# Two transformer layers in one launch: more output products by pairs with seven block products, q and k by tokens, transposes later

## The chip, the cores and the metric

The program runs on one core of a Trainium2 chip. The metric is the device time of one launch in microseconds (us). Inputs and the result are f32 in HBM; every weight is read once.

## The reference, cut to what matters

A hybrid layer and then a second layer, for 256 tokens of width 2048:

```
proj = rms_norm(x, g_mix) @ w_in            # qa, ka, va, qr, kr, vr, gr, gate_a, gate_r
oa   = attention(rms_norm(heads(qa), q_gain), rms_norm(heads(ka), k_gain), heads(va))   # 8 heads of 128
orr  = head_group_norm(retention(qr, kr, vr)) * silu(gr)                                # 4 heads
merged = sigmoid(gate_a) * (oa @ w_o_attn) + sigmoid(gate_r) * (orr @ w_o_ret)
x = x + merged @ w_out
g, u = split(rms_norm(x, g_ffn) @ w_ffn_in)           # 2 x 5632
x = x + (silu(g) * u) @ w_ffn_out
# second layer
x = x + rms_norm(token_mixer(rms_norm(x)), attn_post_norm)
a, b = split(rms_norm(x) @ w_ffn_in_2)                # 2 x 5632
x = x + rms_norm((gelu(conv3(a)) * b) @ w_ffn_out_2, ffn_post_norm)
```

## The kernel before, in words

Every large product is made in three parts: an f32 operand is split into a high part (a rounded copy, type f32r) and a low part (the rest), and high x high, high x low and low x high are added in PSUM. Activations are kept split and transposed (`hx1`, `orr`, `mg`, `hx2`, `act`, `hx3`, `hx4`). Weights come from HBM by SyncE in blocks of 128 x 1024 (512 KB) through four buffers (`wraw`), and each block is split on its way: ScalarE copies the high part (L113), VectorE subtracts it for the low part (L115). `Sched` does this in the order of the tasks: each task calls `take()` once a block, which loads six blocks and splits four blocks ahead of TensorE. After each block comes `tick()`: it runs what `later(n, ...)` has put n steps ahead, and one step of each of two lists of generators (attention, retention and the like). So the whole order of the work on every engine is written out at build time, and each engine keeps that order.

Kinds of tasks: **V** takes a block of 256 rows of weights x 512 columns with the activations as stationary operand and makes two token tiles of 512 columns, 12 products of 512 columns a block (L1261 to L1263). **T** takes the weights as stationary operand and makes 128 features of all tokens, so a product of 512 columns (high and low of the activations side by side) and one of 256 for each 128 rows (L1388, L1390). **B** and **W** keep the blocks' parts and do one token tile after the other, with other work hung between the blocks ("hooks"); W has 256 columns a product. **S** (`pair_products`) takes two groups of 512 columns, left and right, at a time: four accumulators `c11` to `c22`. A block in the order with mark `True` uses a scheme with 7 products of 128-row blocks in place of 8: `p1`, `p5`, `p6`, `p7` are four more accumulators in the other four PSUM banks, sums of activations (`comb`) meet sums of weights, which VectorE makes from the two raw blocks in `sums()` (four operations of 512 columns, L145 to L149) and which are split like a block. Only the first FFN's input product (`w_f1`, 11 pairs with 3 such blocks each, order `ORDER`) is of this kind.

PSUM has eight banks, four under the tag `acc` and four under `m`. A pair's accumulators come from one tag and the four `p` from the other, by turns.

Around the change: `qk_evac` takes q's and k's features, makes their squares, and a step later `stats()` sums them with products of one column (L535); `attention()` makes the factors from it, spreads k's over 128 partitions with two transposes a head (`bcast`, L426) and scales k. `turned()` transposes row tiles `wait` steps after it is called (2 if nothing is said), four 128 x 128 transposes (L465) a half. `x4_row`, `x4_turn`, `x4_low` are the hooks that add the second mixer's result to x (VectorE), transpose it (TensorE, then four high parts on ScalarE) and make the low parts (VectorE). The FFNs' 44 row tiles go in two parts, `PARTS` = groups 0 to 5 and 6 to 10: input product, then output product of those groups, added into `x1` (`row_add`) or `ff` (`f_out`). The last output group of the second FFN is made as W over the second part (20 rows of weights of 128), so that the first token tile's result can be finished under the second one's products (`out_row`).

Large activations live in 15 slots of 8 KB a partition; `t512` has six buffers of 512 columns.

Of the kernel before, what the change touches and what calls it, by code (L numbers as in the profile page):

```python
# [11 lines left out]
F32 = mybir.dt.float32  # L12
# [14 lines left out]
PARTS = ((0, 6), (6, NG))  # L27
# [201 lines left out]
def body(ctx, tc, A, out):  # L229
# [141 lines left out]
    def pair_blocks(arr, a, b, order):  # L371

        blks = []
        for c, seven in order:
            left, right = [arr[g, c].rearrange("p a b -> p (a b)") for g in (a, b)]
# [3 lines left out]
    def pairs_of_groups(arr, of, order, lhs, comb, gate, done, first):  # L379

        blks = [b for x, y in of for b in pair_blocks(arr, x, y, order)]
        tasks.append(("S", blks, (len(of), order, lhs, comb, gate, done, first)))
# [84 lines left out]
    def turned(key, f0, srcs, use=None, then=None, gain=None, wait=2, comb=()):  # L467

        def part(j):
            def fn():  # L470
                m = mtile()
# [22 lines left out]
    def combine(key, i, m, gain):  # L494

        y, s = t512("y"), t512("s4")
        for n in range(2):
            copy(y[:, cols(n, S)], m[:, cols(n, S)], gain[n])
        a11, a21, a12, a22 = [y[:, cols(n, P)] for n in range(4)]
# [8 lines left out]

    def comb_of(key):
        return lambda i, n: st[("comb", key)][i // 2][:, i % 2, :, cols(n, P)]  # L510


    hx1 = rhs_of("hx1")

# [5 lines left out]
    st["qks"] = None  # L520

    def qk_evac(key, f, base):
        def evac(acc):
            y = st[key][:, f]
            total(y, acc)
            yield "post"
            sq = tmp.tile([P, S], F32, name="sq", tag="sq", bufs=2)
            nc.scalar.activation(sq, y, AF.Square)

            def stats():  # L530
                if st["qks"] is None:
                    st["qks"] = mtile()
                for k in range(2):
                    c = base + 2 * f + k
                    nc.tensor.matmul(st["qks"][:, c:c + 1], sq[:, k * P:(k + 1) * P], ones[:, 0:1],  # L535
                                     start=True, stop=True)
            q.later(1, stats)
        return evac
# [18 lines left out]
    for f in range(8):  # L557
        T(A["w_qa"], f, hx1, qk_evac("qa", f, 0))
    for f in range(8):
        T(A["w_ka"], f, hx1, qk_evac("ka", f, 16))  # L560

    def attention():
        yield
        yield
        r = nx.r
        r2 = small(2, "r2")
        tt(r2, r, r, ALU.mult)
        f32t = small(32, "qkf", 1)
        ms = small(32, "qkm", 1)
        tt(pairs(ms, 16), pairs(st["qks"][:, :32], 16), r2[:, None, :].to_broadcast([P, 16, 2]), ALU.mult)  # L570
        root(f32t, ms, 128)
        gqk = small(1, "gqk", 1)
        stt(gqk, gains["qk_norm"][:, 0:1], SC128, gains["qk_norm"][:, 1:2], ALU.mult, ALU.mult)
        yield
        yield
        tt(pairs(f32t, 16), pairs(f32t, 16), r[:, None, :].to_broadcast([P, 16, 2]), ALU.mult)
        yield
        st["oa"] = [slot([P, 4, 2, S], F32R, name="oa") for _ in range(2)]
        for h in range(A_HEADS):
            m = bcast(f32t[:, 16 + 2 * h:18 + 2 * h])  # L580
            kh = t256("kh")
            stt(kh, st["ka"][:, h], gqk, m[:, :S], ALU.mult, ALU.mult)
            yield
            p, rs = yield from softmax_rows(st["qa"][:, h], kh, f32t[:, 2 * h:2 * h + 2], -(2.0 ** -(h + 1)))
# [115 lines left out]
    def gr_evac(g):  # L700
        def evac(accs):
# [7 lines left out]
            turned("orr", 4 * g, sg, wait=1)  # L709
        return evac  # L710

    C(lambda: new_h("orr"))
# [14 lines left out]
    def ret_out(g):  # L727
        def evac(accs):
# [4 lines left out]
            turned("mg", 4 * g, sr)  # L733
        return evac

    C(lambda: new_h("mg"))
    for g in range(4):
        V(A["w_ga"], g, hx1, gate_evac("sa", AF.Sigmoid, nx))
        V(A["w_gret"], g, hx1, gate_evac("sr", AF.Sigmoid, nx))
# [25 lines left out]
    SEVEN = (0, 1, 2)  # L765
# [6 lines left out]

    for a, b in PARTS:
        C(lambda n=b - a: new_h("act", n))
        pairs_of_groups(A["w_f1"], [(j, NG + j) for j in range(a, b)], ORDER, rhs_of("hx2"), comb_of("hx2"), n1, "act",
                        (b - a) % 2)
# [298 lines left out]
    def x4_low(k, g):  # L1075
# [4 lines left out]
        (1, 0): [more], (1, 1): [(x4_row, 0, 0)], (1, 2): [(x4_turn, 0, 0), more], (1, 3): [(x4_row, 0, 1), (x4_low, 0, 0)],  # L1080
        (1, 4): [(x4_turn, 0, 1), more], (1, 5): [(x4_row, 0, 2), (x4_low, 0, 1)], (1, 6): [(x4_turn, 0, 2), more],
        (1, 7): [(x4_row, 0, 3), (x4_low, 0, 2)]}, cs=MIX)
    x4_hooks = {
        (0, 0): [(x4_turn, 0, 3)], (0, 1): [(x4_low, 0, 3)], (0, 2): [(x4_row, 1, 0)],
        (0, 3): [(x4_turn, 1, 0), (x4_row, 1, 1)], (0, 4): [(x4_low, 1, 0), (x4_turn, 1, 1)],
        (0, 5): [(x4_row, 1, 2), (x4_low, 1, 1)], (0, 6): [(x4_turn, 1, 2), (x4_row, 1, 3)],
# [42 lines left out]
    def f2_evac(key, j, use, then):  # L1129
# [63 lines left out]
    for a, b in PARTS:  # L1193
# [7 lines left out]
        if a == 0:  # L1201
            C(start_ff)
# [329 lines left out]
```

## Time and profile before

| | us |
|---|---|
| three runs | 2743.81, 2744.10, 2744.53 (median 2744.1) |
| profiled execution | 2742.58, of which the span 2740.8 |
| TensorE busy | 2708.5 (99%), 12777 matmuls |
| VectorE busy | 1689.7 (62%) |
| ScalarE busy | 1355.4 (49%) |
| DMA | mean 187 GB/s |

Busy time of TensorE is made of matmuls that overlap, their ends are modelled. Start-to-start times on its timeline tell what one costs. "Idle before" and "waits" count only time in which the engine had nothing running.

### The profile page before, as it was taken

What the parts mean: (1) busy time and instruction counts of PE and PEld (TensorE: products, weight loads), DVE (VectorE), ACT (ScalarE), POOL (GpSimd) and SP (SyncE); (2) the same over time, 40 slices, a digit from 0 to 9 for tenths busy, and PEclk for the clock granted to TensorE, in tenths of its full rate; (3) what the DMA queues carried; (4) which work ended last, traced back from release to release, by engine and by line L of the source; (5) the groups of instructions that cost most, each with busy time, mean ns of one, the idle gap of its engine ahead of it and who ended that gap; (6) DMA issues with size and microseconds to landing.
All of it is one profiled execution on the core that took longest, in us unless ns stands there. A gap on an engine that the chain in (4) does not pass through costs nothing.

```text
span 2740.8 us, 33567 instructions
## 1 busy us (share of the span) xinstructions
PE 2708.5 (99%) x12777; PEld 2253.2 (82%) x12777; DVE 1689.7 (62%) x2033; ACT 1355.4 (49%) x1759; POOL 59.5 (2%) x61
## 2 busy tenths in 40 slices
PE   8999999999999999999999999999999999999998
PEld 7888788888888887888888888888778888888887
DVE  5456555554467898648886557775555554455555
ACT  5445444444455555435555455554455554455543
POOL 0000000000000000000000001110000000000000
PEclk9999999999999999999999999999999999999999
DMA  8554456555555555655656565445555555555554
GB/s 276 175 181 163 160 171 215 194 189 196 191 177 195 179 200 191 209 194 182 207 184 204 183 210 168 145 152 191 177 177 184 185 185 191 192 191 185 185 189 142
DMA packets 142227, 511.42 MB, mean 187 GB/s; under 512 B 16945, under 2 KB 17329, under 8 KB 141553
## 3 DMA queue, kind: packets, MB, share of 16 engines
q1 hardware_dynamic: 140832, 502.71, 55.6%
q0 software_dynamic: 1088, 6.55, 0.6%
q8 instruction: 100, 1.64, 0.2%
q14 instruction: 63, 0.51, 0.1%
q10 hardware_dynamic: 144, 0.01, 0.0%
HBM read 507.11 MB, written 2.10 MB: 186 GB/s over the span
## 4 chain that ended last, share of the span: by engine, by line
PE 82%; DVE 8%; DMA 4%; issue 3%; ACT 2%; POOL 0%; DVEq 0%; ACTq 0%; POOLq 0%
PE acc L1263 21%; PE acc L1261 21%; PE acc L1262 21%; PE acc L1388 8%; DVE wlo L115 4%; PE acc L1390 4%; DMA wraw<-in_w_f 3%; PE m L465 1%; ACT whi L113 1%; DVE u L277 1%; PE acc L1286 1%; PE acc L1287 1%; PE acc L1288 1%; DVE sums L145 1%; DVE sums L146 1%
## 5 line engine op out<-in xcount | busy, mean ns | idle before, releaser
L115 DVE TENSOR_TENSOR wlo<-wraw,whi 128x1024 fp32r<-128x1024 f32 (+1 forms) x934 | 1119.3, 1206 | 802.6 <-ACT whi L113 798.7
L113 ACT ACTIVATE whi<-wraw 128x1024 fp32r<-128x1024 f32 (+1 forms) x934 | 966.6, 1041 | 788.3 <-PE acc L1263 675.0
L1261 PE MATMUL acc<-whi,hx 128*128 128x512 f32 x1456 | 581.7, 400 | 7.1 <-ACT hx L274 5.3
L1262 PE MATMUL acc<-wlo,hx 128*128 128x512 f32 x1456 | 568.4, 390 | 1.2 <-DVE wlo L115 1.2
L1263 PE MATMUL acc<-whi,hx 128*128 128x512 f32 x1456 | 569.3, 391 | 0.0
L1388 PE MATMUL acc<-hx,whi 128*128 128x512 f32 x912 | 330.6, 404 | 0.0
L1261 PEld LDWEIGHTS acc<-whi,hx 128*128 128x128 f32 x1456 | 274.0, 188 | 64.3 <-ACT hx L274 5.3
L1262 PEld LDWEIGHTS acc<-wlo,hx 128*128 128x128 f32 x1456 | 274.2, 188 | 58.8 <-DVE wlo L115 2.4
L1263 PEld LDWEIGHTS acc<-whi,hx 128*128 128x128 f32 x1456 | 273.8, 188 | 58.5
L1261 PE MATMUL acc<-whi,act 128*128 128x512 f32 (+1 forms) x704 | 271.1, 385 | 0.0
L1263 PE MATMUL acc<-whi,act 128*128 128x512 f32 (+1 forms) x704 | 269.8, 383 | 0.0
L1262 PE MATMUL acc<-wlo,act 128*128 128x512 f32 (+1 forms) x704 | 269.8, 383 | 0.0
L1390 PE MATMUL acc<-hx,wlo 128*128 128x256 f32 x912 | 255.7, 280 | 0.0
L1388 PEld LDWEIGHTS acc<-hx,whi 128*128 128x128 f32 x912 | 171.3, 188 | 38.9 <-issue 0.5
L1390 PEld LDWEIGHTS acc<-hx,wlo 128*128 128x128 f32 x912 | 172.4, 189 | 1.0 <-issue 0.5
L1263 PEld LDWEIGHTS acc<-whi,act 128*128 128x128 f32 x704 | 132.3, 188 | 26.1
L1261 PEld LDWEIGHTS acc<-whi,act 128*128 128x128 f32 x704 | 132.3, 188 | 25.7
L1262 PEld LDWEIGHTS acc<-wlo,act 128*128 128x128 f32 x704 | 132.4, 188 | 25.4
L113 ACT ACTIVATE whi<-sums 128x1024 fp32r<-128x1024 f32 x66 | 68.9, 1057 | 112.6 <-DVE sums L146 72.9
L1286 PE MATMUL m<-whi,hx 128*128 128x512 f32 x291 | 113.8, 391 | 0.0
L1288 PE MATMUL m<-whi,hx 128*128 128x512 f32 x291 | 113.3, 389 | 0.0
L1287 PE MATMUL m<-wlo,hx 128*128 128x512 f32 x291 | 113.3, 389 | 0.0
(332 smaller groups left out, 3047.9 us busy)
## 6 DMA issues: line engine op xcount, KB each, us to landing
wraw<-in_w_f SPq DMA_DIRECT2D x352, 512.0 KB, 3.4
wraw<-in_w_f1o SPq DMA_DIRECT2D x88, 512.0 KB, 4.2
wraw<-in_w_f2o SPq DMA_DIRECT2D x78, 512.0 KB, 3.3
wraw<-in_w_ga SPq DMA_DIRECT2D x34, 512.0 KB, 3.3
wraw<-in_w_vr SPq DMA_DIRECT2D x32, 512.0 KB, 3.3
wraw<-in_w_gr SPq DMA_DIRECT2D x32, 512.0 KB, 3.3
wraw<-in_w_gret SPq DMA_DIRECT2D x32, 512.0 KB, 3.9
wraw<-in_w_or SPq DMA_DIRECT2D x32, 512.0 KB, 3.3
```

Source lines behind the costliest of these rows:

```text
L113: nc.scalar.activation(hi[:, c], raw[:, c], AF.Copy)
L115: nc.vector.tensor_tensor(lo[:, c], raw[:, c], hi[:, c].bitcast(F32), op=ALU.subtract)
L145: tt(t1, b12, b11, op=ALU.subtract)
L146: tt(t3, b22, b12, op=ALU.subtract)
L1261: nc.tensor.matmul(accs[k], x[:, 0], hi[:, w], start=b, stop=False)
L1262: nc.tensor.matmul(accs[k], x[:, 0], lo[:, w], start=False, stop=False)
L1263: nc.tensor.matmul(accs[k], x[:, 1], hi[:, w], start=False, stop=e)
L1286: nc.tensor.matmul(acc, x[:, 0], hi, start=start, stop=False)
L1287: nc.tensor.matmul(acc, x[:, 0], lo, start=False, stop=False)
L1288: nc.tensor.matmul(acc, x[:, 1], hi, start=False, stop=stop)
L1388: nc.tensor.matmul(acc, hi[:, w], x.rearrange("p a b -> p (a b)"), start=(k == first), stop=False, skip_group_check=True)
L1390: nc.tensor.matmul(acc[:, S:], lo[:, w], x[:, 0], start=False, stop=(k == last), skip_group_check=True)
```

## The change

The gates of the first layer (3 of 4 groups: left `w_ga`, right `w_gret`), the first FFN's output product and all but the last part of the second FFN's output product go through `pair_products`, with some blocks of seven products. The sums of activations for these (`combine_later`) are made by a generator, from the split parts. What `pair_products` does with its accumulators is now in classes (`Gates`, `Gated`, `Added`, `Begun`). The second FFN goes in three parts, and W covers the last one only (12 rows). q and k become V tasks; their squares are summed by ScalarE, k is scaled by rows on VectorE, and both are transposed. `turned` gets `wait=3` in the FFNs and takes its bank from the tag that is free; the hooks of x4 are moved.

```diff
-PARTS = ((0, 6), (6, NG))
+PARTS = ((0, 5), (5, NG))
+PARTS_2 = ((0, 4), (4, 8), (8, NG))
+    def combine_later(key, cs):
+        st[("comb", key)] = []
+        for i, c in enumerate(cs):
+            y = t512("y")
+            x = st[key][c // 2][:, 2 * c % 4:2 * c % 4 + 2].bitcast(F32)
+            tt(pairs(y), x[:, :, 0], x[:, :, 1], ALU.add)
+            yield
+            sums_of(key, i, y)
+            yield
+    def qk_evac(key, g, base):
+        def evac(accs):
+            y = [t512("qk") for _ in range(2)]
+            for k in range(2):
+                copy(y[k], accs[k])
+            yield "pre"
+            for k in range(2):
+                for h in range(4):
+                    c = base + 2 * (4 * g + h) + k
+                    nc.scalar.activation(junk[:, :P], y[k][:, cols(h, P)], AF.Square, accum_out=qks[:, c:c + 1])
+            if base:
+                yield "pre"
+                c = slice(base + 8 * g, base + 8 * g + 8)
+                head_norms(c)
+                yield "pre"
+                times_r(c)
+                for k in range(2):
+                    f = qkf[:, c].rearrange("p (h k) -> p h k", k=2)[:, :, k:k + 1]
+                    tt(pairs(y[k], 4), pairs(y[k], 4), f.to_broadcast([P, 4, P]), ALU.mult)
...
+            turned(key + "_t", 4 * g, y, use, wait=3)
-    for f in range(8):
-        T(A["w_qa"], f, hx1, qk_evac("qa", f, 0))
+    for g in range(2):
+        V(A["w_qa"], g, hx1, qk_evac("qa", g, 0), when=lambda: nx.ready)
...
+    class Gates:
+        def both(self, key, accs, y):
+            for k in range(2):
+                tt(y[k], accs[k], y[k], ALU.add)
+            for k in range(2):
+                nc.scalar.activation(y[k], y[k], AF.Sigmoid, scale=nx.r[:, k:k + 1])
+            st[key] = y
...
+    PAIRED = (0, 1, 2)
+    ORDER_G = [(3, False), (4, False), (0, True), (5, False), (1, True), (6, False), (2, True), (7, False)]
+        if g in PAIRED:
+            pairs_of_groups([((A["w_ga"], g), (A["w_gret"], g))], ORDER_G, hx1, comb_of("hx1"), Gates(), 1)
...
+    SEVEN_A = (0, 1)
+    def order_out(a, b, cs):
+        plain = [c for c in range(b * 2 - a * 2) if c not in cs]
+        step = 2 if len(plain) > 6 else 1
+        order = []
+        for i, c in enumerate(plain):
+            order.append((c, False))
+            if i >= 2 and (i - 2) % step == 0 and (i - 2) // step < len(cs):
+                order.append((cs[(i - 2) // step], True))
+        return [(2 * a + c, seven) for c, seven in order]
+    class Added:
+        def put(self, g, accs, v, tile):
+            rows = [y[:, cols(g)] for y in st[self.key]]
+            for k in range(2):
+                tt(v[k], accs[k], v[k], ALU.add)
+                tt(rows[k], rows[k], v[k], ALU.add)
+            if self.norm is None:
+                return
+            for k in range(2):
+                self.norm.feed(rows[k], k, g)
+            turned("hx3", 4 * g, rows, gain=lambda f: gains["attn_pre_norm_2"][:, f:f + 1], wait=3, tile=tile)
...
-        for g in range(4):
-            V(A["w_f1o"], g, lambda k, a=a: rhs_of("act")(k - 4 * a),
-              row_add("hx3", g, n2 if a else None, "attn_pre_norm_2"), cs=range(2 * a, 2 * b))
+        cs = SEVEN if a else SEVEN_A
+        C(lambda cs=cs: q.work[0].append(combine_later("act", cs)))
+        pairs_of_groups([((A["w_f1o"], g), (A["w_f1o"], g + 1)) for g in (0, 2)], order_out(a, b, cs),
+                        lambda k, a=a: rhs_of("act")(k - 4 * a), comb_of("act"),
+                        Added("x1", n2 if a else None), 1)
...
-        (1, 0): [more], (1, 1): [(x4_row, 0, 0)], (1, 2): [(x4_turn, 0, 0), more], (1, 3): [(x4_row, 0, 1), (x4_low, 0, 0)],
+        (1, 0): [more], (1, 1): [(x4_row, 0, 0)], (1, 2): [(x4_row, 0, 1), more], (1, 3): [(x4_turn, 0, 0), (x4_row, 0, 2)],
...
-            turned(key, 4 * j, scaled("ab", accs, n3), use, then)
+            turned(key, 4 * j, scaled("ab", accs, n3), use, then, wait=3, tile=tile)
...
+            C(lambda: q.work[0].append(combine_later("act", SEVEN_A)))
+            pairs_of_groups([((A["w_f2o"], g), (A["w_f2o"], g + 1)) for g in (0, 2)], order_out(a, b, SEVEN_A),
+                            lambda k, a=a: rhs_of("act", 5)(k - 4 * a), comb_of("act"),
+                            Added("ff", None) if a else Begun("ff", None), 0)
-    W(A["w_f2os"], range(4 * PARTS[1][0], 4 * NG), lambda k: act_row(k - 4 * PARTS[1][0]), f_last, f_tile,
-      {(1, g): [(out_row, 0, g)] for g in range(4)})
+    W(A["w_f2os"], range(4 * end, 4 * NG), lambda k: act_row(k - 4 * end), f_last, f_tile,
+      {(1, 0): [(out_row, 0, 0)], (1, 1): [(out_row, 0, 1), (out_row, 0, 2)], (1, 2): [(out_row, 0, 3)]})
```

## Rows read from the trace of the kernel before

**Rows 1.** The page, parts 1 and 2: engines, slices, granted clock.

```profile
PE 2708.5 (99%) x12777; PEld 2253.2 (82%) x12777; DVE 1689.7 (62%) x2033; ACT 1355.4 (49%) x1759; POOL 59.5 (2%) x61
...
DVE  5456555554467898648886557775555554455555
...
PEclk9999999999999999999999999999999999999999
```

**Rows 2.** Waits of TensorE: us in total, times, longest.

```profile
PE m L465 <- DVE x L283: 7.3, 6, 2.2
...
PE acc L1287 <- DVE wlo L115: 2.5, 5, 0.8
PE m L465 <- ACT ab L274: 1.9, 2, 1.7
...
PE m L465 <- DVE g L283: 1.2, 4, 0.3
...
PE m L1287 <- DVE wlo L115: 0.9, 3, 0.3
```

**Rows 3.** Windows (length; busy PE, PEld, DVE, ACT): gates, pairs, x after mixer, output.

```profile
496.35:573.48 77.13, 77.13 (x346) 63.85 (x345) 39.41 (x36) 33.22 (x34) 0.00 (x0) 1.00 0.57 191
924.87:967.88 43.01, 42.73 (x192) 35.02 (x191) 38.92 (x47) 23.88 (x28) 0.00 (x0) 1.00 0.58 195
1965.40:2000.00 34.60, 27.26 (x131) 21.04 (x131) 23.99 (x50) 17.32 (x42) 1.12 (x2) 1.00 0.40 132
2262.60:2394.10 131.50, 131.50 (x585) 108.89 (x584) 61.39 (x52) 56.63 (x58) 0.00 (x0) 1.00 0.58 193
```

**Rows 4.** The same, of one tile's products: a V group, W.

```profile
507.23:528.99 21.76, 21.76 (x96) 17.83 (x95) 0.00 (x0) 0.00 (x0) 1.00 0.58 194
2703.10:2731.82 28.72, 28.72 (x241) 28.64 (x239) 0.00 (x0) 0.00 (x0) 1.00 0.28 93
```

**Rows 5.** Timeline of TensorE, q's products: start us, us, instruction.

```profile
64.25 0.28 PE L1390 MATMUL acc<-hx,wlo 128*128 128x256 f32 x1
64.37 0.50 PE L535 MATMUL m<-ones,sq 128*128 128x1 f32 x4
...
65.05 0.28 PE L1390 MATMUL acc<-hx,wlo 128*128 128x256 f32 x1
...
70.46 0.50 PE L535 MATMUL m<-ones,sq 128*128 128x1 f32 x4
```

**Rows 6.** The same: a spread of k's factors, and a set of transposes.

```profile
170.33 0.28 PE L1390 MATMUL acc<-hx,wlo 128*128 128x256 f32 x1
170.45 0.38 PE L426 MATMUL m<-c_ident,qkf 128*128 128x128 f32 x2
...
170.90 0.29 PE L1390 MATMUL acc<-hx,wlo 128*128 128x256 f32 x1
...
2106.01 0.39 PE L1263 MATMUL acc<-whi,hx 128*128 128x512 f32 x1
2106.24 0.60 PE L465 MATMUL m<-c_ident,ab 128*128 128x128 f32 x4
...
2106.91 0.40 PE L1262 MATMUL acc<-wlo,hx 128*128 128x512 f32 x1
```

**Rows 7.** The same: the first transposes of the second FFN.

```profile
2015.47 0.39 PE L1263 MATMUL acc<-whi,hx 128*128 128x512 f32 x1
2017.55 0.33 PE L465 MATMUL m<-c_ident,ab 128*128 128x128 f32 x1 [1.70 <-ACT ab L274]
```

**Rows 8.** VectorE by line (busy us, mean ns): splits, sums of weights.

```profile
L115 DVE TENSOR_TENSOR wlo<-wraw,whi 128x1024 fp32r<-128x1024 f32 x48 | 58.8, 1226 | 69.1 <-ACT whi L113 69.1
...
L149 DVE TENSOR_TENSOR sums<-wraw,sums 128x512 f32<-128x512 f32 x3 | 2.1, 692 | 0.1
```

**Rows 9.** Timeline of VectorE at the end.

```profile
2724.79 0.42 DVE L277 TENSOR_TENSOR ff<-acc,ff 128x256 f32<-128x256 f32 x1 [3.97 <-PE acc L1263]
...
2726.98 2.74 DVE L283 SCALAR_TENSOR_TENSOR ff<-ff,r_f,x 128x512 f32<-128x512 f32 x4 [0.45 <-POOL r_f L419]
```

More of the change, by code (lines that the diff above doesn't have):

```diff
@@ L465, in turn, with turned @@
                 nc.tensor.transpose(m[:, (i * len(srcs) + k) * P:][:, :P], src[:, (n * j + i) * P:][:, :P], ident)
-    def turned(key, f0, srcs, use=None, then=None, gain=None, wait=2, comb=()):
+    def turned(key, f0, srcs, use=None, then=None, gain=None, wait=2, comb=(),
+               tile=mtile):
         def part(j):
             def fn():
-                m = mtile()
+                m = tile()
                 turn(m, srcs, j)
@@ L513, in body, with free_sums @@
     hx1 = rhs_of("hx1")
+    SEVEN = (0, 1, 2)
+    def free_sums():
+        q.mixed = None
     def alloc(key, shape, n=None, dt=F32):
@@ L770, in body, with turn_act, __init__, last @@
         V(A["w_out"], g, rhs_of("mg"), row_add("hx2", g, n1, "norm_ffn", SEVEN))
+    def turn_act(f0, rows, tile):
+        for j in range(2):
+            m = tile()
+            turn(m, rows, j)
+            f = f0 + 2 * j
+            h_tile("act", f)
+            dst = st["act"][f // 4][:, f % 4:f % 4 + 2]
+            split(dst[:, :, 0], dst[:, :, 1], pairs(m))
+    class Gated:
+        def __init__(self, count):
+            self.count = count
+        def last(self, n, shared):
+            if n:
+                turn_act(4 * (n - 1), self.rows, shared)
+        def left(self, n, accs, g, own):
+            for k in range(2):
+                tt(g[k], accs[k], g[k], ALU.add)
+            for k in range(2):
+                nc.scalar.activation(g[k], g[k], AF.Silu, scale=n1.r[:, k:k + 1])
+            self.rows = g
+        def right(self, n, accs, u, own):
+            g = self.rows
+            for k in range(2):
+                tt(u[k], accs[k], u[k], ALU.add)
+            for k in range(2):
+                stt(g[k], u[k], n1.r[:, k:k + 1], g[k], ALU.mult, ALU.mult)
+            if n == self.count - 1:
+                turned("act", 4 * n, g, wait=3, tile=own)
@@ L1189, in start_ff, with load_post, put @@
         st["ff"] = [slot([P, D], name="ff") for _ in range(2)]
+    def load_post():
         st["post"] = slot([P, D], name="post")
         nc.gpsimd.dma_start(st["post"], A["ffn_post_norm_2"])
-    for a, b in PARTS:
+    class Begun(Added):
+        def put(self, g, accs, v, tile):
+            for k in range(2):
+                tt(st[self.key][k][:, cols(g)], accs[k], v[k], ALU.add)
+    end = PARTS_2[-1][0]
+    for a, b in PARTS_2:
         C(lambda n=b - a: (new_h("act", n), new_h("conv", 0)))
@@ L1288, in three, with pair_products @@
         nc.tensor.matmul(acc, x[:, 1], hi, start=False, stop=stop)
-    def turn_act(key, f0, rows, tile):
-        for j in range(2):
-            m = tile()
-            turn(m, rows, j)
-            f = f0 + 2 * j
-            h_tile(key, f)
-            dst = st[key][f // 4][:, f % 4:f % 4 + 2]
-            split(dst[:, :, 0], dst[:, :, 1], pairs(m))
-    def pair_products(count, order, lhs, comb, norm, key, first):
+    def pair_products(count, order, lhs, comb, after, first):
         sevens = [i for i, (c, seven) in enumerate(order) if seven]
-        prev = None
         for n in range(count):
@@ L1345, in pair_products @@
                     if e:
-                        if prev is not None:
-                            turn_act(key, 4 * (n - 1), prev, shared)
-                        for k, acc in enumerate((c11, c21)):
-                            tt(g[k], acc, g[k], ALU.add)
-                        for k in range(2):
-                            nc.scalar.activation(g[k], g[k], AF.Silu, scale=norm.r[:, k:k + 1])
+                        after.last(n, shared)
+                        after.left(n, (c11, c21), g, own)
                     q.tick()
@@ L1360, in pair_products @@
                     if e:
[L1361 to L1365 removed]
+                        after.right(n, (c12, c22), u, own)
                 q.drain(ACC_BUFS)
                 q.tick()
[L1368 removed]
     for kind, blks, what in tasks:
```

162 lines of the change are left out of this document (87 added, 75 removed).

## The prediction

> **What bounds the kernel now.** I read the page's engine lines first: TensorE is busy for 2708.5 of 2740.8 us and its granted clock stands at the upper level of 2.4 GHz in every slice [rows 1]. So the time is the sum of TensorE's instructions, and an edit is worth the products that it takes away plus the stalls that it takes away, as long as VectorE, which prepares the weights, keeps up. Then TensorE's own waits: they are few, and five of them belong to lines that the change touches [rows 2]. Then the windows by stage, to see how near VectorE is to its limit: about half busy in the gates, 47% in the output products of the second FFN, but 38.92 of 43.01 us in the one stage that already works by pairs [rows 3]. Last the timeline of TensorE, for the price of single things. A matmul's record lasts 0.39 us, but the next one starts 0.227 us later, so the price of a product is start to start: 96 products take 21.76 us, 0.2267 each [rows 4]. For the same reason an idle time that follows a product hides about 0.16 us of what it really costs (0.39 less 0.227).
>
> **The change, part by part.** Durations are of the profiled execution, 2742.6 us; the median of the runs is 2744.1, which is 1.5 more.
>
> *Seven products.* A block of a pair has 24 matmuls (2 token tiles x 2 rows of weights x 2 groups x 3); one with seven products has 21. New blocks of this kind: gates 3 groups x 3 = 9; first FFN's output 2 pairs x 2 in its first part and 2 x 3 in its second = 10; second FFN's output 2 parts x 2 pairs x 2 = 8. That is 27 blocks, 81 matmuls, 81 x 0.2267 = 18.4 us off. The 33 such blocks of the first FFN's input stay.
> The Trainium skill ("TensorE: Matmul & The Clock Gate", Back-to-back issue gap) gives two spacings for 512 columns: about 131 ns in a sustained stream of loads and products, and 512/2.4 + 2.5, about 216 ns, for the isolated gap. By these the 81 products would bring 10.6 or 17.5 us, and the sum below would be 24.6 or 31.5. This case's stream runs at 227 ns [rows 4], so neither is used.
>
> *q and k by tokens.* Before, a tile of 128 features takes one 512-column and one 256-column product for each of 16 rows of weights, and then four tiny statistics products; two such groups stand 6.09 us apart [rows 5], so 16 tiles take 97.4 us. By tokens the same weights are 4 x 96 products of 0.2267, 87.0 us. Gain 10.4, the statistics (0.45 a tile, 64.25 to 65.05 less one pair of products) included. Added: 4 groups x 2 sets of four transposes; such a set holds the products up by 0.90 - 2 x 0.227 = 0.45 us [rows 6], 8 x 0.45 = 3.6. Removed: the spread of the factors, two transposes a head, 0.57 - 0.35 = 0.22 us [rows 6], 8 heads, 1.8. Net 8.6 off. The new work elsewhere (ScalarE's copies and squares, VectorE's scaling, POOL's root) has three steps of about 2.7 us to finish before the transposes; VectorE is half idle there, from the second slice on [rows 1], so I cost it at nothing; without that cover each of the eight sets could wait for about one such 0.69 us operation, 5 us in all. The attention loop starts where it did, with one step fewer a head.
>
> *Transposes behind their rows, at the end of the second layer's mixer.* Six waits, 7.3 us, stand on the transposes of x [rows 2]: with 6 x 0.16 this is 8.3 us. Each transpose is issued one hook after the vector operation that makes its row, and that operation stands behind a split of weights. Now the row is made two hooks ahead. Of the 34.6 us of this stretch VectorE works 23.99 [rows 3]; with all 8.3 gone it would be busy 24.0 of 26.3, 91%, and it also waits there on ScalarE. So something will be late, either a low part or a split. Bounds 3.6 (two waits as long as the longest, 2.2 + 0.16, stay) and 8.3; I take 6.3, near the upper one since the queue itself is not full.
> *Three steps instead of two* for the FFN's transposes: the two waits on ab are 1.9 us, with 2 x 0.16 2.2; the first alone holds TensorE from 2015.47 to 2017.55, 1.85 us over a product [rows 2, 7]. One more step is 2.7 us, so all 2.2 go. The four waits on g, 1.2 us and with 4 x 0.16 1.9, go in the same way: the last group's transposes move one step on, and now start from other columns. What is late next is nothing that the trace shows.
>
> *The last product by halves* shrinks from 20 rows of weights to 12: 240 products of 256 columns at 28.72/240 = 0.12 become 144 (28.7 to 17.2), and 8 rows go to the pairs, 48 x 0.2267 = 10.9 [rows 4]. Off 0.6. Against it: the second token tile then takes 36 x 0.12 = 4.3 us. VectorE takes from the first sum at 2724.79 to 2729.72 for the first token's rows [rows 9], 4.9 us, and the second token's sum is queued behind them. On: 0.6.
>
> *What VectorE gets.* A seven block needs three full splits at 1.23, half a one at about 0.69 and four sums at 0.69 [rows 8], 7.1 us, against 21 x 0.2267 = 4.8 on TensorE; a plain block 2.5 against 5.4. With the orders given, a pair of gates needs 3 x 7.1 + 5 x 2.5 = 34 us plus eight 0.69 operations, 39 of 41.5 us. The tightest is the first pair of the second FFN's second part: 2 x 7.1 + 6 x 2.5, four sums, eight additions, the sums of two activation blocks (an estimate of 2.6 each from the same row) and the last group's gating: 45 against 42.2 us. Splits run up to four steps ahead, 4 x 2.7 us, and the stage ahead of each new pair stage leaves VectorE half idle, so that the 3 us are covered. In the present pair stage the waits on the split are 2.5 + 0.9 us in eight [rows 2], with 8 x 0.16 4.7 us for 33 blocks, 0.14 a block. 27 x 0.14 = 3.8; below, nothing, if the lead is always full; I take 3, since here more plain blocks stand between.
> *Switches.* Seven new pair tasks take all eight banks, and with entry and exit make 14 switches at which a product wants a bank that VectorE has still to read. At the tightest (the first FFN's sums) three operations of 0.69 have 2.7 us; one split ahead of them makes it 0.6 late. Bounds 0 and 14 x 0.6 = 8.6; I take 2, as the present pair stage and the three-way hand-over around it show no such wait in [rows 2].
>
> Sum: 18.4 + 8.6 + 6.3 + 2.2 + 1.9 + 0.6 = 38.0 off; 0.6 + 3 + 2 = 5.6 on; net 32.4. From 2742.6 that is 2710.2, in terms of the median 2711.7: I say 2711.
>
> **Rivals.** *A: VectorE becomes the bound in the new pair stages, slower.* If the lead of four splits is used up (by the new sums of activations, the additions that now stand in VectorE's queue right after the products, ScalarE's squares waiting for them), each new seven block costs TensorE what VectorE lacks: 7.1 - 4.8 = 2.3 us, 27 x 2.3 = 63 on. 38 less 3: slower by about 28, 2772. It turns from gain to loss at 38/27 = 1.4 us a block. For it: 38.92 of 43.01 us in the present stage. Against: there the same blocks stand closer and cost 0.14 each.
> *B: the switches cost.* Every one of the 14 waits the 0.6 us and twice that where the additions of two groups meet, 12 us more than I take: 2723. For it: all eight banks in use, and half of the pairs begin right behind an evacuation. Against: [rows 2] has no wait on an evacuated bank.
> The Trainium skill ("Perfetto Trace Analysis", Optimization Strategy) says that a gap that keeps repeating on the engine that should be full can mean too little SBUF or PSUM for the next tile. In the trace of before no such gap recurs; if B holds, one will stand at each switch.
> *C: the moved work isn't gained:* the transposes of x wait for VectorE as before, and q's and k's transposes wait too: 6.3 + 5 less, 2722.
>
> **How the numbers follow.** Forecast 70%, with a range of its own from 2704 (no new waits, all of the 8.3 us: 32.4 + 3 + 2 + 2 = 39.4 off) to 2728 (x at 3.6, switches at 8.6, the splits at 10, well above the 3.8: 32.4 - 2.7 - 6.6 - 7 = 16.1 off). B 14%, C 10%, both inside that range; A 6%, of which the part past the turning point is slower. The range 2704 to 2728 thus leaves out A and the far ends. About 0.2%, 5.5 us, is what a measurement of this kernel can tell from no change: faster 0.91, same 0.04, slower 0.05.
>
> **What would show it.** PE's matmul count of 512 columns by three lines of the seven products: 81 fewer in the three stages; no L535 line; q and k in 87 us and eight sets of transposes. Gate groups with pairs some 2.0 us shorter (9 x 0.2267). In TensorE's waits: x below 2.5 us, ab and g gone, the split of a seven block below 8 us in all. Wrong would be: VectorE over 95% in a stage of gates or output products with TensorE waiting on the split; a wait on a bank at the start of a stage; a total that moved by less than 15 us.

## The result and the profile after

| | before | after |
|---|---|---|
| median of four runs, same chip | 2744.06 (2743.81 to 2744.53) | 2711.23 (2709.74 to 2714.07) |
| profiled execution, its span | 2742.58, 2740.8 | 2712.53, 2710.8 |

The ratio is 0.9881 [0.9864, 0.9899]: 32.8 us off the median, 30.0 off the profiled span. 2711 was predicted. A second timing of the same kernel, e12 below, gave 0.9892 [0.9877, 0.9907]. The total is right, but some of its terms are wrong, and in part they cancel.

The page after, parts 1 and 2 (answers to [rows 1]):

```profile
PE 2681.7 (99%) x12472; PEld 2224.1 (82%) x12472; DVE 1873.3 (69%) x2349; ACT 1411.6 (52%) x1876; POOL 60.5 (2%) x63
...
DVE  5455566777467898889888857775565685568555
...
PEclk9999999999999999999999999999999999999999
```

TensorE is still full and, as the mean of each slice, at the upper level of its clock; VectorE has 184 us more to do, and two slices at 90% or more, where it had one. TensorE's waits after (us in total, times, longest), beside [rows 2]:

```profile
PE acc L1415 <- ACT hx L275: 5.3, 1, 5.3
PE m L1441 <- DVE wlo L116: 2.9, 4, 1.2
PE acc L1441 <- DVE wlo L116: 2.9, 4, 1.1
PE acc L1416 <- DVE wlo L116: 1.8, 3, 0.8
PE m L1440 <- ACT whi L114: 1.6, 1, 1.6
PE acc L1415 <- ACT whi L114: 1.4, 1, 1.4
PE acc L466 <- DVE g L284: 1.3, 4, 0.4
PE m L466 <- DVE th L284: 1.1, 1, 1.1
PE m L466 <- DVE x L284: 1.0, 1, 1.0
```

x has gone from 7.3 to 1.0 and ab is no longer there; g has stayed (1.2, now 1.3); the first product of a block of weights now also waits once for ScalarE's high part, for 1.6 us. No wait is on a bank of PSUM. (L1440 to L1442 are the three products of a pair's block, L1415 to L1417 those of a plain one, L466 a transpose, L114 and L116 the split.)

The time by stage, from the start of the first large product of one stage to that of the next:

| stage | before | after | e12 | predicted change |
|---|---|---|---|---|
| q and k, qr and kr, vr and gr (with the attention beside them) | 395.97 | 387.17 | 387.14 | -8.6 |
| gates | 308.51 | 304.53 | 303.17 | -6.1 |
| first FFN, input product | 472.47 | 471.65 | 471.34 | 0 |
| first FFN, output product | 246.32 | 245.14 | 243.82 | -6.8, and -1.9 for g |
| start of the second layer (`dv`) | 44.74 | 45.62 | 45.62 | 0 |
| second mixer's output and second FFN's input product | 600.80 | 590.00 | 589.99 | -6.3 and -2.2 |
| second FFN's output product, with W | 251.92 | 248.05 | 247.64 | -5.4 |

The stages left out moved by 1.4 us together, 1.2 of it in the opening one, whose length is 54.6 to 55.9 us in the executions here, whatever the edit. Against these the prediction had 5 us of new stalls, 3 for splits and 2 for switches, spread over the stages of pairs. The windows of five stages after, and of the first pair of the second FFN's second output part (us, then busy PE, PEld, DVE, ACT, POOL, the granted clock, DMA share, GB/s):

```profile
54.64:144.56 89.92, 89.92 (x410) 74.41 (x408) 41.26 (x38) 51.08 (x95) 2.56 (x1) 1.00 0.56 186
441.81:746.34 304.53, 303.55 (x1350) 250.01 (x1349) 207.38 (x221) 149.41 (x159) 1.10 (x2) 1.00 0.60 200
1052.82:1161.89 109.07, 107.79 (x478) 88.50 (x476) 87.34 (x106) 53.64 (x57) 0.00 (x0) 1.00 0.57 196
1417.93:1554.01 136.08, 132.25 (x584) 108.13 (x582) 110.57 (x138) 70.82 (x87) 0.00 (x0) 0.99 0.56 189
2146.54:2232.11 85.57, 85.57 (x381) 70.45 (x380) 70.89 (x87) 43.51 (x47) 0.00 (x0) 1.00 0.57 193
2412.91:2455.75 42.84, 42.84 (x193) 35.03 (x192) 35.45 (x48) 22.83 (x26) 0.00 (x0) 1.00 0.51 170
```

In q and k and in the second FFN's output TensorE never stands still by its records. Most of what was lost is in the fourth line, the second part of the first FFN's output: 3.8 us idle by the records, although VectorE is busy for 81% there, less than in the second FFN's output (83%), which loses nothing. So VectorE's total doesn't explain it. The three engines' timelines at that place (start, us, instruction, and in brackets the idle time before it and its releaser), first TensorE:

```profile
1441.93 0.39 PE L1442 MATMUL m<-whi,comb 128*128 128x512 f32 x1
1443.95 0.50 PE L1440 MATMUL m<-whi,act 128*128 128x512 f32 x1 [1.63 <-ACT whi L114]
1445.21 0.79 PE L1441 MATMUL m<-wlo,act 128*128 128x512 f32 x1 [0.76 <-DVE wlo L116]
1445.80 0.63 PE L1442 MATMUL m<-whi,act 128*128 128x512 f32 x1
```

ScalarE, which had the high part to make:

```profile
1437.31 0.63 ACT L273 ACTIVATE comb<-s 128x512 fp32r<-128x512 f32 x1 [4.61 <-DVE s L278]
1437.85 1.05 ACT L114 ACTIVATE whi<-sums 128x1024 fp32r<-128x1024 f32 x1
1438.80 0.61 ACT L114 ACTIVATE whi<-wraw 128x512 fp32r<-128x512 f32 x1
1442.32 0.63 ACT L273 ACTIVATE comb<-s 128x512 fp32r<-128x512 f32 x1 [2.91 <-DVE s L278]
1442.86 3.88 ACT L114 ACTIVATE whi<-wraw 128x1024 fp32r<-128x1024 f32 x4
```

and VectorE:

```profile
1440.67 0.68 DVE L116 TENSOR_TENSOR wlo<-wraw,whi 128x512 fp32r<-128x512 f32 x1
1441.28 0.28 DVE L278 TENSOR_TENSOR s<-y 128x128 f32<-128x128 f32 x1
...
1442.01 0.28 DVE L278 TENSOR_TENSOR s<-y,s 128x128 f32<-128x128 f32 x1
1442.98 0.69 DVE L278 TENSOR_TENSOR comb<-s,comb 128x512 fp32r<-128x512 f32 x1 [0.70 <-ACT comb L273]
1443.93 4.63 DVE L116 TENSOR_TENSOR wlo<-wraw,whi 128x1024 fp32r<-128x1024 f32 x4 [0.25 <-ACT whi L114]
```

Read from the bottom of ScalarE's rows: four copies of whole blocks of weights, without idle time between them, run right behind the copy `comb<-s`, which is the high part of a sum of activations. That copy stood in ScalarE's queue for 2.91 us until VectorE had made `s`, and the copies of weights stood behind it. Then VectorE stands still for 0.70 us until the copy is there, with its own splits of weights behind. Both engines wait for each other in turn, and TensorE for both.

Something else stands at this place. After TensorE's two waits, of 1.63 and 0.76 us, its products start 0.43 us apart instead of 0.227 for a while, without idle time, and the granted clock of that stretch is 0.52, the lower level of 1.2 GHz. In e12, the same kernel with the same two waits (1.62 and 0.77), it stays at 1.00:

```profile
1446.23 0.63 PE L1440 MATMUL m<-whi,act 128*128 128x512 f32 x1
...
1445.60:1448.80 3.20, 3.20 (x9) 2.48 (x9) 2.96 (x3) 1.28 (x3) 0.00 (x0) 0.52 0.67 210
...
1444.72:1447.92 3.20, 3.20 (x16) 2.63 (x15) 3.01 (x3) 1.34 (x3) 0.00 (x0) 1.00 0.80 253
```

The first two lines are after's, the last is e12's. Eight products take 3.53 us from 1445.21 to 1448.74, and the same eight 1.95 in e12, so the lower clock costs 1.6 us; the stage is 136.08 in after and 134.98 in e12, which loses 0.5 more on g. Why the clock falls in one execution and not in the other is open.

The order of the queues was theory **Q** before the experiments on it; theory **V** was that VectorE's added work itself is too much for the stage.

### The profile page after: what moved, and what is told of

Same layout as the page of the kernel before. It is cut to its first block, busy times and chain, and to the rows that moved or that the text cites. A ratio compares the mean times of both kernels' runs of the same rounds, so it can differ in the third digit from the quotient of the medians.

```text
span 2710.8 us, 33386 instructions
## 1 busy us (share of the span) xinstructions
PE 2681.7 (99%) x12472; PEld 2224.1 (82%) x12472; DVE 1873.3 (69%) x2349; ACT 1411.6 (52%) x1876; POOL 60.5 (2%) x63
## 4 chain that ended last, share of the span: by engine, by line
PE 87%; DVE 7%; DMA 3%; ACT 2%; issue 1%; DVEq 0%; ACTq 0%; POOLq 0%; POOL 0%
PE acc L1417 16%; PE acc L1415 16%; PE acc L1416 16%; PE acc L1522 6%; PE m L1441 4%; PE m L1442 4%; PE m L1440 4%; PE acc L1441 4%; PE acc L1442 4%; PE acc L1440 4%; DVE wlo L116 3%; PE acc L1524 3%; DMA wraw<-in_w_f 2%; PE m L466 2%; ACT whi L114 1%
## 5 line engine op out<-in xcount | busy, mean ns | idle before, releaser
L116 DVE TENSOR_TENSOR wlo<-wraw,whi 128x1024 fp32r<-128x1024 f32 (+1 forms) x936 | 1101.0, 1190 | 595.4 <-ACT whi L114 588.5
L114 ACT ACTIVATE whi<-wraw 128x1024 fp32r<-128x1024 f32 (+1 forms) x936 | 951.4, 1028 | 626.0 <-PE acc L1417 396.0
L1415 PE MATMUL acc<-whi,hx 128*128 128x512 f32 x1392 | 555.7, 399 | 6.7 <-ACT hx L275 5.3
L1416 PE MATMUL acc<-wlo,hx 128*128 128x512 f32 x1392 | 542.9, 390 | 1.1 <-DVE wlo L116 1.1
L1417 PE MATMUL acc<-whi,hx 128*128 128x512 f32 x1392 | 543.7, 391 | 0.0
L1415 PEld LDWEIGHTS acc<-whi,hx 128*128 128x128 f32 x1392 | 262.0, 188 | 60.6 <-ACT hx L275 5.3
L1417 PEld LDWEIGHTS acc<-whi,hx 128*128 128x128 f32 x1392 | 261.7, 188 | 55.9
L1522 PE MATMUL acc<-hx,whi 128*128 128x512 f32 x656 | 238.6, 405 | 0.0
L114 ACT ACTIVATE whi<-sums 128x1024 fp32r<-128x1024 f32 x120 | 126.2, 1059 | 191.8 <-DVE sums L147 119.1
L1524 PE MATMUL acc<-hx,wlo 128*128 128x256 f32 x656 | 183.4, 280 | 0.0
L116 DVE TENSOR_TENSOR wlo<-sums,whi 128x1024 fp32r<-128x1024 f32 x120 | 146.6, 1222 | 14.8 <-ACT whi L114 11.8
L1440 PE MATMUL m<-whi,hx 128*128 128x512 f32 x386 | 151.2, 392 | 0.0
L1442 PE MATMUL m<-whi,hx 128*128 128x512 f32 x386 | 150.3, 389 | 0.0
L1524 PEld LDWEIGHTS acc<-hx,wlo 128*128 128x128 f32 x656 | 123.8, 189 | 1.1 <-issue 0.5
L1440 PE MATMUL acc<-whi,hx 128*128 128x512 f32 x300 | 117.3, 391 | 0.0
L1442 PE MATMUL acc<-whi,hx 128*128 128x512 f32 x300 | 116.8, 389 | 0.0
L1441 PE MATMUL acc<-wlo,hx 128*128 128x512 f32 x300 | 116.8, 389 | 0.0
L1440 PE MATMUL m<-whi,act 128*128 128x512 f32 x259 | 101.8, 393 | 1.6 <-ACT whi L114 1.6
L1441 PE MATMUL m<-wlo,act 128*128 128x512 f32 x259 | 101.7, 393 | 0.8 <-DVE wlo L116 0.8
```

The costliest lines, as they stand in the source:

```text
L114: nc.scalar.activation(hi[:, c], raw[:, c], AF.Copy)
L116: nc.vector.tensor_tensor(lo[:, c], raw[:, c], hi[:, c].bitcast(F32), op=ALU.subtract)
L1415: nc.tensor.matmul(accs[k], x[:, 0], hi[:, w], start=b, stop=False)
L1416: nc.tensor.matmul(accs[k], x[:, 0], lo[:, w], start=False, stop=False)
L1417: nc.tensor.matmul(accs[k], x[:, 1], hi[:, w], start=False, stop=e)
L1440: nc.tensor.matmul(acc, x[:, 0], hi, start=start, stop=False)
```

## The experiments

Each is the kernel after with one edit. The kernel before differs by chip (2737.4 to 2744.1), so ratios are to the before of the same chip: 2739.60 for e1 to e4, 2737.44 for e5 to e8, 2738.77 for e9 to e12. Stage times are from the profiled execution of each.

### One part undone: e1 to e5

**e1, gates without pairs.**

```diff
...
-    C(lambda: q.work[1].append(combine_later("hx1", SEVEN)))
...
-    PAIRED = (0, 1, 2)
+    PAIRED = ()
```

> The gates are again two plain groups each; everything else as after (2711.2). Theory (products): 9 blocks x 3 matmuls x 0.2267 = 6.1 us more by the products; the stage in the traces became only 4.0 us shorter, so about 2715. Rival A (VectorE eats the saving in the new pair stages): no change or shorter, 2711 or less.

2718.91 (2718.21 to 2720.26), 0.9926 [0.9911, 0.9941]. The gates take

```profile
442.94:751.42 308.48, 308.48 (x1378) 255.38 (x1377) 156.53 (x143) 134.63 (x138) 1.10 (x2) 1.00 0.57 198
```

against 304.53 after and 302.69 to 304.51 in the other runs that have the pairs (e9 apart): they are worth 4.0 to 5.8 of the 6.1 predicted. After has two stalls there, 0.3 and 1.0 us over a product's spacing, at 646 and 647 us, where the products with `w_oa` give way to those with `w_or`; the executions with 302.7 are without the larger part of that. The total lost more than the stage: in this profile the second part of the first FFN's input was also 2.8 us longer than after, for which the edit gives no reason; so the price of the edit is read from the stage.

**e2, first FFN's output product without pairs.** Parts 0 to 5 and 6 to 10 as before, and four V tasks in place of two pairs:

```diff
-PARTS = ((0, 5), (5, NG))
+PARTS = ((0, 6), (6, NG))
...
-        pairs_of_groups([((A["w_f1o"], g), (A["w_f1o"], g + 1)) for g in (0, 2)], order_out(a, b, cs),
...
+        for g in range(4):
+            V(A["w_f1o"], g, ...
```

> The first FFN's output product by plain groups, in the two parts of before (6 and 5 groups). Products alone: 10 blocks x 0.68 = 6.8 us more, 2718. The traces show that stage only 1.2 us shorter and its neighbour 0.9 longer, so if the two traces are right the pairs bring nearly nothing here: 2711 to 2713. Rival A would say 2711 or less.

2711.74 (2710.60 to 2712.11), 0.9898 [0.9882, 0.9915], 1.7 to 4.7 us above what the two ratios of after give on this chip, and the intervals are that wide. The two stages take 133.00 and 113.33, together 246.33 as before; the pairs have 1.2 (after) or 2.5 (e12) less, of which 0.9 comes back in `dv`. Ten blocks of seven that should bring 6.8 bring next to nothing.

**e3, second FFN's output product without pairs.**

```diff
...
-            pairs_of_groups([((A["w_f2o"], g), (A["w_f2o"], g + 1)) for g in (0, 2)], order_out(a, b, SEVEN_A), ...
+            for g in range(4):
+                V(A["w_f2o"], g, lambda k, a=a: rhs_of("act", 5)(k - 4 * a), f_part(g, a), cs=range(2 * a, 2 * b))
```

> The second FFN's output product by plain groups, still in three parts with W over the last. Products alone: 8 blocks x 0.68 = 5.4 us more, 2716.6; the trace of after shows almost no stall there (0.4 us a stage), so I expect the whole of it. Rival A: no change.

2714.58 (2713.00 to 2717.18), 0.9911 [0.9896, 0.9926]. Both stages take 88.00:

```profile
2142.60:2230.60 88.00, 88.00 (x393) 72.88 (x392) 41.77 (x36) 39.65 (x42) 0.00 (x0) 1.00 0.55 191
```

With pairs they take 85.38 and 85.41 in e12, 5.2 us less, for 24 products that should bring 5.4. Where the stage has no stall at all (85.28 in e10) the 12 products are worth 88.00 - 85.28 = 2.72, 0.2267 each: the spacing of [rows 4] to the digit. The Trainium skill ("TensorE: Matmul & The Clock Gate", Back-to-back issue gap) gives about 216 ns for 512 columns as the isolated gap and about 131 ns in a sustained stream; by these the estimate for 12 products is 2.59 or 1.57 us. The measurement decides: 227 ns here.

**e4, q and k by features**, as before (`qk_evac`, the statistics and the spread of k's factors put back; T tasks in place of V).

> q and k by features as before, everything else as after. Theory: 10.4 + 1.8 - 3.6 = 8.6 us more, 2719.8 (the three stages from q to gr are 8.8 shorter in the traces). Rival C (the moved work is not gained): 2711 to 2714.

2721.08 (2718.64 to 2721.85), 0.9932 [0.9917, 0.9947]. The first of its three stages against the 89.92 after:

```profile
54.70:151.84 97.14, 97.14 (x573) 85.11 (x572) 46.61 (x48) 44.07 (x64) 0.00 (x0) 1.00 0.52 177
```

All three together are 395.97, as before to the hundredth, and 8.8 us above after. The transposes of q and k wait for nothing: no such line is in the waits after.

**e5, the hooks of x4 as before** (only the two tables of hooks; the rows are made one hook ahead again).

> The hooks of x after the second mixer in the order of before; everything else as after (2711.2). Theory: the waits on x return, 8.3 us against the 1.2 that the trace of after keeps: 7.1 more, 2718.3. Rival C (VectorE is full there, the order gives nothing): 2711 to 2713.

2716.19 (2715.10 to 2718.15), 0.9923 [0.9908, 0.9938]. The wait is back,

```profile
PE m L466 <- DVE x L284: 7.4, 6, 2.1
```

and the stages are 93.24 and 187.93 against 89.33 and 184.51: the move is worth 7.3 us, of the 8.3 that the prediction had as its upper bound.

### The first FFN's output: e6 to e8, e10, e11

**e6, transposes four steps behind.** The g transposes wait although `wait` went from 2 to 3. What after's trace shows at the end of the input pairs:

```profile
1052.82 0.39 PE L1440 MATMUL m<-whi,act 128*128 128x512 f32 x1
...
1058.04 0.39 PE L1442 MATMUL m<-whi,act 128*128 128x512 f32 x1
1058.67 0.33 PE L466 MATMUL acc<-c_ident,g 128*128 128x128 f32 x1 [0.24 <-DVE g L284]
1059.33 0.55 PE L466 MATMUL acc<-c_ident,g 128*128 128x128 f32 x3 [0.33 <-DVE g L284]
```

The first row is the first product after the pair; 24 products (5.44 us) later come the transposes, exactly as many as before. The call of `turned` now stands ahead of the block's own `tick()`, where it stood behind one, so three steps are the former two.

```diff
-                turned("act", 4 * n, g, wait=3, tile=own)
+                turned("act", 4 * n, g, wait=4, tile=own)
```

> The last group's transposes of each part of the first FFN one step later than in after (wait 4). Theory: in after the call comes ahead of the block's own step, so wait 3 is the same 24 products as before and the four waits on g stayed; one more step takes 2.7 us and they go: 1.9 to 2.1 less, 2709.2. Rival: something else in that chain is late and they move along: no change.

2710.12 (2708.11 to 2711.03), 0.9901 [0.9885, 0.9918]: no faster. The waits on g are gone, but the two stages take 108.92 and 134.79, as in e12 (108.85 and 134.97). The time is lost at a wait for ScalarE's high part instead, which stands neither in after nor in e12:

```profile
PE acc L1440 <- ACT whi L114: 1.7, 2, 1.2
```

It is 0.5 us in the first stage and 1.2 in the second, where e12 has 0.3 and 1.3 on g. A stall that only hides a later one is worth nothing when it is removed alone.

**e7, the blocks of seven one place later** in the order of the output product.

```diff
...
-            if i >= 2 and (i - 2) % step == 0 and (i - 2) // step < len(cs):
+            if i >= at and (i - at) % step == 0 and (i - at) // step < len(cs):
```

> In the first FFN's output product the first block of seven products comes one plain block later (after four instead of three). In after 4.9 us of stalls stand in the first pairs of that stage, at the weights' splits. Theory L (VectorE's and ScalarE's lead is empty there, because the stage follows the busiest one, and the sums of activations use up what is left): one plain block gives back 3 us of VectorE, stalls fall to about 2: 3 less, 2708. Rival S (a bank at the switch): the stall stands at the same product, no change. Rival A (bound for good): no change, the stall moves along.

With `at=3`: 2710.49 (2709.70 to 2711.12), 0.9901 [0.9887, 0.9916]. The expectation missed: the stages are 107.77 and 135.46, 1.1 better than in e12 and no better, and `dv` is 1.2 longer. The wait on the high part is gone, and in its place stand

```profile
PE m L466 <- DVE x L278: 3.0, 4, 1.0
...
PE acc L1415 <- DVE g L278: 0.8, 1, 0.8
```

transposes of x, and a product of `dv` whose bank VectorE has still to read. With the kernel's own work this is the one place where rival B's mechanism shows: 0.8 us idle and 0.16 hidden, between the 0.6 and the 1.2 that B gave a switch. (e9 shows another.)

**e8, no sums of activations** in the first FFN's output. Its blocks of seven take those of the input product instead, so the result is another.

```diff
...
-        C(lambda cs=cs: q.work[0].append(combine_later("act", cs)))
...
-                        lambda k, a=a: rhs_of("act")(k - 4 * a), comb_of("act"),
+                        lambda k, a=a: rhs_of("act")(k - 4 * a), comb_of("hx2"),
```

> The sums of activations for the first FFN's output product are left out: its seven-product blocks take those of the product before as a stand-in (this part of the result is then another). Theory L, and within it that the sums (their splits queue on ScalarE ahead of the weights') are the cause: the 4.9 us of stalls go, 2706.3. Rival S or A: 2710 to 2711, stalls remain.

2703.55 (2701.96 to 2705.76), 0.9877 [0.9862, 0.9892]. The second stage:

```profile
1416.87:1547.58 130.71, 129.73 (x584) 107.09 (x582) 104.41 (x121) 69.88 (x85) 0.00 (x0) 1.00 0.58 198
```

5.4 us less than after and 4.3 less than e12, whose clock didn't fall, with VectorE only 6.2 us less busy. So the sums of activations are the cause of the waits; whether by their work (V) or by their place (Q), this run can't say.

**e10, the split one step after the sums.** The same instructions, but the copy `comb<-s` and VectorE's subtraction behind it are issued one step later, so that VectorE has a step more to make `s`:

```diff
...
-            sums_of(key, i, y)
+            s = sums_of(key, i, y, True)
+            yield
+            halves(st[("comb", key)][i // 2][:, i % 2], s)
```

> The split of the activations' sums is issued one step after the sums, so that ScalarE's copy of it no longer waits in its queue for VectorE with the weights' copies behind it. Theory Q (the queue order costs, three times 0.7 us of idle VectorE and the copies behind): the first FFN's second output stage falls from 136 to 133 or 134, 2 to 3 us less in all. Theory V (VectorE's work itself is too much there): less than 0.5.

2704.49 (2703.55 to 2706.53), 0.9875 [0.9860, 0.9890]; the unaltered kernel on the same chip (e12) is at 2709.45, and the ranges don't touch. The stage, in e10

```profile
1417.83:1548.74 130.91, 129.73 (x583) 107.08 (x582) 110.67 (x139) 71.10 (x88) 0.00 (x0) 1.00 0.58 198
```

and in e12

```profile
1416.58:1551.56 134.98, 130.62 (x584) 106.93 (x582) 110.73 (x139) 70.75 (x87) 0.00 (x0) 1.00 0.56 191
```

VectorE does the same 110.7 us of work in both, and TensorE gets 4.1 us back (1.1 more in the first part). Neither execution has the fall of the clock. ScalarE's line of these copies, over the whole run (busy us, mean ns, idle before), says why; after:

```profile
L273 ACT ACTIVATE comb<-s 128x512 fp32r<-128x512 f32 x15 | 9.5, 632 | 44.7 <-DVE s L278 44.7
```

and e10:

```profile
L273 ACT ACTIVATE comb<-s 128x512 fp32r<-128x512 f32 x15 | 9.4, 629 | 14.0 <-DVE s L278 13.9
```

Q holds, with a gain of 5.0 us, above the 2 to 3 it had forecast. The two stages of e10 take 107.75 + 130.91 = 238.66 us, with all the work in them, and those of e8, without the sums, 238.56: as work the sums cost TensorE nothing. The edit moves the copy on ScalarE and the subtraction on VectorE together; which of the two queues weighed more was not separated.

**e11, the sums on POOL** as well, with e6's fourth step.

```diff
...
+        add = (lambda o, a, b, op: nc.gpsimd.tensor_tensor(o, a, b, op=op)) if later else tt
...
-        tt(s1, a21, a22, ALU.add)
+        add(s1, a21, a22, ALU.add)
...
```

> As e10, and the sums of activations (one addition of 512 columns, four of 128) go from VectorE to POOL, and the last group's transposes wait 4 steps. Theory V: VectorE loses 1.9 us a block where it was the bound, the stalls at the splits go as without the sums (4.9 us), and then the later transposes pay their 2: 6 to 7 us less than after, ratio 0.986. Theory Q alone: 2 to 3 us less. Rival: POOL's operations slow VectorE's, or come too late for the first block: no gain or worse.

2704.08 (2702.18 to 2705.28), 0.9872 [0.9857, 0.9887]: 0.4 us from e10, no difference that can be told. The work taken off VectorE is worth nothing measurable once the order is right; V's 6 to 7 us are not there. The waits on g are gone in this trace, and its two stages take 237.61, 1.05 less than e10's; whether the fourth step brings this, now that nothing later is hidden behind g, or POOL does, was not separated.

**e12, the kernel after again**, for the same chip.

> The changed kernel once more, unaltered, beside the three others on one chip. Before differed between chips by 6 us (2744.1, 2739.6, 2737.4); if its ratio to before is a property of the kernels, it is 0.988 again.

2709.45 (2709.35 to 2709.62), 0.9892 [0.9877, 0.9907]. e10 and e11, at 2704.5 and 2704.1, beat both kernels.

### How near rival A was: e9

One of the four sums of weights is made three times, 2 x 0.69 us of VectorE more for each of the 60 blocks of seven.

```diff
             tt(t1, b12, b11, op=ALU.subtract)
+            tt(t1, b12, b11, op=ALU.subtract)
+            tt(t1, b12, b11, op=ALU.subtract)
```

> Each of the 60 blocks of seven products makes its first sum of weights three times instead of once: 2 x 0.69 = 1.4 us more for VectorE a block, nothing else. Rival A (VectorE bounds all pair stages): 60 x 1.4 = 83 us more. Theory (VectorE bounds only the first FFN, where it is 90% busy and no slack is built up between its pairs; the gates and the second FFN's output product have slack): nothing in the gates and the second FFN; the first FFN's 33 input blocks lose what is over 42.4 us a pair, 11 x about 2 = 22, the 10 output blocks about 10: 30 us more in all.

2774.64 (2772.92 to 2776.99), 1.0133 [1.0116, 1.0150], 65 us above e12 for 83 us of work. The first part of the first FFN's input and the first of the second FFN's output:

```profile
841.30:1076.04 234.74, 219.14 (x956) 173.70 (x955) 209.62 (x255) 117.91 (x139) 1.08 (x1) 1.00 0.53 178
2201.40:2289.66 88.26, 86.50 (x381) 70.37 (x380) 75.32 (x94) 43.39 (x47) 0.00 (x0) 1.00 0.53 183
```

with e12's for comparison:

```profile
836.39:1051.18 214.79, 213.36 (x956) 175.33 (x955) 189.82 (x226) 119.61 (x139) 1.08 (x1) 1.00 0.58 194
...
2144.04:2229.42 85.38, 85.38 (x381) 70.53 (x380) 70.81 (x87) 43.51 (x47) 0.00 (x0) 1.00 0.58 193
```

In the input product the 33 blocks lose 44.1 us, 1.34 each of the 1.38 added. The expectation of nothing elsewhere missed: the second FFN's output loses 5.9 (0.73 a block), the first's 7.2, the gates 5.0, although VectorE is busy for only 75.32 of 88.26 us in the second FFN's. A share of 83% over the stage (e12) thus hides stretches in which there is no slack. Of the gates' 5.0, 2.4 is one wait on a bank, rival B's mechanism again: a product with `w_oa` waits for ScalarE's copy out of a pair's bank (`PE acc L1417 <- ACT g L275: 2.4, 1, 2.4`).

## Why the prediction came out right, and where it was wrong

**What bounds the kernel**: right. TensorE stayed full, the granted clock at the upper level but for some 3 us in the first FFN's output (1.6 us lost, in after and not in e12), and products taken away are worth their spacing: e3 and e10 give 0.2267 us each, e1 most of it.

**q and k by tokens**: 8.6 predicted, 8.8 measured (e4), and the three steps of lead cover the added work altogether, as said. **x**: 6.3 predicted between bounds of 3.6 and 8.3; 7.3 measured (e5). The caution ("something will be late") took off 2 where one wait of 1.0 is left. Rival C (2722) therefore didn't come. **ab**: 2.2 predicted, and the line is gone. With x at 7.3, this leaves 1.3 of the 10.8 us of that row of the table; 0.9 of it are two sets of four transposes that the third part moved to the output stages (152 transposes of ab in the input stages, 160 before), the rest is open. **W**: net 0 predicted. From its first product to the end it took 37.82 us before and takes 26.94 now; the 10.88 between them are just what the 48 products cost that moved to the pairs, so net 0.

**Seven products**: right in the gates (4.0 to 5.8 of 6.1) and the second FFN's output (5.2 of 5.4), wrong in the first FFN's output: 1.2 (after) to 2.5 (e12) in place of 6.8, less 0.9 for two sets of transposes of x that moved on to `dv`. The step that failed is the one that costs VectorE's list as work, a sum of durations to be covered by the lead, and puts the order of the two helpers' queues at nothing. In the pair that it held to be the tightest, 45 against 42.2 us, VectorE is busy for 35.45 of 42.84 us (the last line of the windows after), and TensorE lost nothing. What cost was the copy of a sum that waits in ScalarE's queue with the weights' copies behind it, and that needs no full engine: e10, which only issues it later, has all of the work, and its two stages are 246.32 - 238.66 = 7.66 us shorter than before, the 6.8 and the 0.9 together. The sentence that the stage ahead of each new pair stage leaves VectorE half idle doesn't hold here either: ahead of the first FFN's output stands the one stage that [rows 3] show at 38.92 of 43.01 us. But it isn't what cost: e10 has the same stage ahead and loses nothing, and e7, with one plain block more for a lead, gained nothing.

**The stalls**: 3 for splits, spread, and 2 for switches were predicted. No wait at a switch is in the trace after, so rival B (2723) is out; the loss at the splits is mostly in one place, the first FFN's output, and about twice as large (its two stages are 5.2 to 6.5 us longer than without any loss, 1.6 of after's by the clock). **g**: 1.9 predicted, 0 measured. Two errors lie in it: the steps were counted from the number in the call and not from where the call stands against `tick()`, and e6 shows that the wait was a cover for a later stall, so that even its going brings nothing here; with the queues in order it may bring about 1 (e11, not separated).

So the gain had too much in it by 1.9 for g, 4.3 to 5.6 for the first FFN's output, 0.3 to 2.1 for the gates and 0.9 for the transposes that went to `dv`. Against that stand the 5 us put in for stalls, the 1.0 more of x and the 1.2 of the opening stage. The 5 us were meant for losses of this kind, so the net of the seven products, 13.4 predicted and 9.5 to 12.6 measured, is nearer than its terms; that x gave more and that the opening came out short, which no edit touched, is luck. 32.4 was predicted; the medians give 32.8, the profiled execution 30.0 and e12 29.3, so that 2711 against 2711.23 is luck as well.

**Rival A** (2772, 6%) didn't come. e9 shows how near it was, but not its turning point of 1.4 us lost in each of the 27 new blocks: with 1.38 us more for VectorE these lose 5.0 + 7.2 + 5.9 = 18 us, 0.67 each, and two thirds of e9's loss falls on the 33 blocks that the kernel before has too. Those lose 1.34 each; the reason against A, that the present blocks cost only 0.14 each, says what they cost and not how much slack they have.

The Trainium skill ("Perfetto Trace Analysis", Optimization Strategy) reads a repeating gap on the full engine as a possible lack of SBUF or PSUM for the next tile. Here TensorE's idle time in the first FFN's second output stage fell from 4.4 us (e12) to 1.2 (e10) with the same buffers and banks; only the place of two instructions in their queues was changed.

## What to carry to other kernels

An instruction that waits for another engine holds up all that is queued behind it: issue it a step after its input, and put the copies that others wait for ahead of it. When one engine must stay fed, go through the lists of the helpers in their order; a busy share of 80% tells neither that there is slack (e9) nor that there is none (e10). Before counting a removed wait as gain, ask what the engine behind it does with the time, and count steps from where the call stands.

## What was not expected of the hardware

The unaltered kernel before ran at 2737.4 to 2744.1 us on the chips used here, a spread of 0.24%, as large as many edits here: only ratios to the before of the same chip compare.

The granted clock can fall in the middle of a full kernel: after waits of 1.63 and 0.76 us with one product between them it was at the lower level for about 3 us in after, and stayed up in e12; that is 1.6 us of time. A single profile of a stage with such waits can therefore be off by as much; e5 has the fall too (its stage takes 136.00), e6 not (134.79).

And the waits list understates a loss. In the second part of the first FFN's output TensorE is idle for 136.08 - 132.25 = 3.83 us in after and for 130.91 - 129.73 = 1.18 in e10, 2.65 less, but the stage is 5.17 us longer. The 1.6 of the lower clock are most of the difference; the rest is mainly what each of the three waits that e10 hasn't got hides behind the record of the product before it, 0.16 us as the prediction had it. Without the clock, e12 against e10, it is 3.18 us of idle time for 4.07 us of the stage.
